# A fused layer on one core: the mixer's first projection moved ahead of its norm, with later residuals and wider steps in fox

## The chip, the cores and the metric

The kernel runs on one core of one Trainium2 chip. The metric is the device time of one execution in microseconds; lower is better. The engines are called as in the profile: PE (TensorE), DVE (VectorE), ACT (ScalarE), POOL (GpSimd), and SP (SyncE), whose queue issues the DMAs.

## The reference, cut to what matters

One decoder layer over 256 tokens with 2048 features, in float32. A conditioning vector c gives nine rows of 2048 (shift, scale and gate of each of three parts).

```
mod = silu(c) @ ada_w + ada_b                  # sh1 sc1 gt1 sh2 sc2 gt2 sh3 sc3 gt3
ada_in(x, g, shift, scale) = rmsnorm(x, g) * (1 + scale) + shift
x = x + 0.5 * gt1 * swiglu(ada_in(x, g0, sh1, sc1), w_gate0, w_up0, w_down0)    # d_ff 5632
x = x + gt2 * mixer(ada_in(x, g1, sh2, sc2))
x = x + 0.5 * gt3 * swiglu(ada_in(x, g2, sh3, sc3), w_gate1, w_up1, w_down1)
out = rmsnorm(x, final_norm)

mixer(h): one input projection gives, for heads of 128,
  8 heads of forgetting attention ("fox"): softmax(q k / sqrt(128) + cum_i - cum_j, causal) v,
      cum = cumsum(log_sigmoid(f + bias)); then rmsnorm
  8 heads of a gated delta rule ("gdn"): conv of width 4 and silu on q, k, v; q and k of unit length;
      g = -exp(A_log) * softplus(a + dt_bias), beta = sigmoid(b), in chunks of 64, each with a
      triangular solve; then rmsnorm times silu(z)
  o = concat(fox, gdn) @ w_out
```

## The kernel before, in words

**Weights.** All weights are one stream of 5392 tiles of 128x128, read in the order of use as 674 blocks of eight (W.block, W.next). For each block SP issues one DMA of 512 KB (wraw, L121), ACT rounds it to the high half (whi, L123) and DVE makes the low half, raw minus high (wlo, L135). The pools hold four blocks each. A product of one tile with 256 tokens is three matmuls: high by high, high by low, low by high. The activations (hs) are kept in halves too, in features by tokens.

**Stages.** FFN1 is blocks 0 to 263, in two halves of its inner width; each half has a stage for gate and up and a stage for down. The second half's down stage (blocks 232 to 263) has 16 output tiles of 16 products, each into a PSUM tile pd. The function after(j) inside ffn adds such a tile to the residual stream x (residual, two DVE steps, L509 and L510, with the gate's column gh, L507) and, in the second half, adds its squares for the next norm (sumsq_add, ACT and POOL). It is called when LATER products of the next tile are issued. Then come the mixer (input projections, heads, W_out), FFN2 and the final norm.

**Conditioning.** Each of the 140 later conditioning columns costs one DMA of 1 MB (adat, L256) and one DVE reduction (L260). They are dealt out along the weight stream: the table RATE gives, from a block on, how many columns fall due per block.

**A norm.** norm_sums turns the squares into sums per token (matmuls nsum, L323), with a square root on ACT and a few small DVE steps. norm_row puts the inverse root on every partition (matmul nrow, L342). modulate_one makes one of the sixteen h tiles: x g (1 + scale) times the row on DVE (ht, L368), shift and high half on ACT, low half on DVE (L372 or L376). Before the mixer, modulate does the sums and the row and leaves the tiles to h_need, which makes them a few ahead of the projection that uses them. Ahead of FFN2 the class Early does it in another way: during W_out it writes y = x g (1 + scale) into hs, the first products run on y with two more columns that hold the shift's halves (products, 258 columns), the sums and the row are issued among them (step), and root and shift are applied to the result (scaled, L433, with shc, L432). The h tiles for the later products are then made behind (h_upto).

**The mixer's order.** project runs the sixteen products of each item. The first call holds four items, interleaved: the gate columns gt and the key heads 0 to 2 of gdn. gates copies its columns to yr, transposes them (pcol, L811), runs a chain of small DVE steps, cumulates over tokens (prow, L844, and pcum), and writes the rows to DRAM (rowd). They come back on all partitions: four heads at a time for decays (fetch_rows, x<-rowd, L894), or one (row_of, rw<-rowd, L870). decays subtracts the rows (Ln, L902) and takes eight exponentials (L905); keys takes a key head's length and its inner products (pk, pkk, L934 to L941), solve the triangular solves. These chains are Python generators: each yield says for how many microseconds of products the chain rests. After a product, tick credits 0.35 us to every running chain, and a chain is resumed when its rest is used up. So all engines' programs are fixed at build time. fox is such a chain too: mask and logits (fm, L1147; plog), transposes (ppt, L1167), the product with v (pfo), the norm, and a transpose back (pft, L1189). ORDER lists the projections after the first: key heads 3 to 7, then z, v and the heads.

Of the kernel before, what the change touches and what calls it, by code (L numbers as in the profile page):

```python
# [16 lines left out]
P = 128  # L17
# [16 lines left out]
RATE = ((0, 0.5), (24, 0.34), (56, 0.45), (68, 0.06), (112, 0.5), (168, 0.38), (264, 0.0), (284, 0.26), (404, 0.0), (424, 0.125))  # L34
# [7 lines left out]
LATER = 8  # L42
# [107 lines left out]
def layer_kernel(ctx: ExitStack, tc: tile.TileContext, xrow, c, adaw, cols, cst, w, out, order, dbg=None):  # L150
# [204 lines left out]
    plain = hsf[:, : KD * HS].rearrange("p (k i) -> p k i", k=KD)[:, :, : 2 * T].rearrange("p k (q t) -> p k q t", q=2)  # L355

# [7 lines left out]
    def modulate_one(j, g1, sh, r, weave=True):  # L364

        t = pt("ht")
        hl, hh, tt = (run(j, LO), run(j, HI), turns(t)) if weave else (plain[:, j, LO], plain[:, j, HI], t)
# [17 lines left out]
    def modulate(which, m_sh, m_sc):  # L385
        ada_need(max(m_sh, m_sc), KD - 1)
        g1 = gains(which, m_sc, 0, KD)
        r = norm_row(norm_sums())
        hq["next"], hq["one"] = 0, lambda j: modulate_one(
            j, g1[:, j : j + 1], mod[:, m_sh * KD + j : m_sh * KD + j + 1], r, False)  # L390

    class Early:
# [3 lines left out]
        def __init__(self, which, m_sh, m_sc):  # L396
            self.which, self.m_sh, self.m_sc, self.row, self.rstd = which, m_sh, m_sc, None, None

        def y(self, j):
# [8 lines left out]
            A.activation(run(j, HI), turns(x[:, j]), AF.Copy, scale=g)  # L408
            V.scalar_tensor_tensor(run(j, LO), turns(x[:, j]), g, run(j, HI).bitcast(F32), ALU.mult, ALU.subtract)  # L409

        def step(self, k):
# [3 lines left out]
            if k == 4:  # L415
                self.row = norm_row(self.rstd, A.copy)
                g1 = gains(self.which, self.m_sc, 0, KD)
                hq["next"], hq["one"] = 0, lambda j: modulate_one(
                    j, g1[:, j : j + 1], mod[:, self.m_sh * KD + j : self.m_sh * KD + j + 1], self.row)
# [8 lines left out]
        def scaled(self, dst, ps):  # L428
# [4 lines left out]
            V.tensor_tensor(dst, ps[:, :T], self.row, ALU.mult)  # L433
# [181 lines left out]
    def ffn(which, m_gt, early=None):  # L615
        fs = list(range(NF))
        with tc.tile_pool(name=f"hid{which}", bufs=PARTS[which][1] + HIDX) as hp, \
                tc.tile_pool(name=f"more{which}", bufs=1) as more:
            W.more = more if MORE else None
            for half in range(2):  # L620
# [7 lines left out]
                def after(j):  # L628
                    residual(pds.pop(j), j, m_gt, True)
                    if half == 1:  # L630
                        sumsq_add(j)
                        if which == 1:
# [9 lines left out]
                for j in range(KD):  # L642
                    ps = psb("pd")
                    for q, hd in enumerate(hids):
                        if j and q == LATER:
# [77 lines left out]
    norm2 = Early(2, 6, 7)  # L723
# [5 lines left out]
    def mixer():  # L729
        modulate(1, 3, 4)  # L730
# [29 lines left out]
        def project(items):  # L760
# [3 lines left out]
            for i, k in todo:  # L764
                m, n = items[i]
                h_need(k)
                wh, wl = W.next(m, k, n)
                hh, hl = woven(plain[:, k, HI]), woven(plain[:, k, LO])
# [3 lines left out]
                tick(TILE_US)  # L772
            return [p_[:, :T] for p_ in pp]
# [671 lines left out]
```

## Time and profile before

| | |
|---|---|
| time, median of 3 runs | 1943.49 us (1943.44 to 1944.72) |
| the profiled execution's own time | 1943.79 us |
| its span in the trace | 1941.9 us |
| PE, DVE, ACT, POOL busy | 1903.0, 1554.0, 1041.2, 56.8 us |
| mean granted clock of PE | 0.992 |
| last pd matmul of FFN1 starts at | 741.19 us |

A line of the profile's timeline reads: start, duration, engine, line of the kernel, operation, output<-inputs, sizes, count, and in brackets how long the engine was idle before and which instruction ended that idle time. A line of a group reads: busy time, mean ns of one | idle time before them and what ended most of it. A line of the windows reads: from:to, length, then busy time and count of PE, weight loads, DVE, ACT and POOL, then the granted clock, the share of the DMA engines' time, and GB/s. A line of the waits reads: engine, what waited, what it waited for: total us, times, the longest.

### The profile page before, as it was taken

The numbers are of one execution on the slowest core, as the hardware profiler recorded it, in microseconds if no ns is written. First come the engines' busy times: TensorE is split into PE (matmuls) and PEld (weight loads), VectorE is DVE, ScalarE is ACT, GpSimd is POOL, SyncE is SP. The second block draws the span as 40 slices with busy tenths as digits, with TensorE's granted clock in tenths as the row PEclk, the third lists the DMA queues.
The fourth block names the chain that finished last, engine by engine and source line by source line (L and its number), as shares of the span: only waits on it lengthen the run. The fifth ranks groups of instructions, "written<-read, shape, count | busy, mean of one in ns | idle before, by whom it ended". The sixth has DMA issues, their size and how long they took to land. (4 is left out here: it accounts for less than half of the span.)

```text
span 1941.9 us, 33701 instructions
## 1 busy us (share of the span) xinstructions
PE 1903.0 (98%) x13087; PEld 1777.2 (92%) x13087; DVE 1554.0 (80%) x2415; ACT 1041.2 (54%) x1647; POOL 56.8 (3%) x55
## 2 busy tenths in 40 slices
PE   8999999999999999999999999999999999999998
PEld 6999999998999988889989998999999999999997
DVE  6999978989989997779987989976777665666654
ACT  6544555433455446858657655665554445555553
POOL 0000000000000030000000001100000000000011
PEclk8999999999999999999999999999999999999999
DMA  9989867999999975586667568667767665565663
GB/s 371 359 308 358 305 224 258 400 369 376 356 358 339 361 302 212 212 314 220 214 242 257 201 218 303 208 258 252 245 253 257 244 225 200 201 200 202 202 200 120
DMA packets 129490, 519.58 MB, mean 268 GB/s; under 512 B 18217, under 2 KB 21545, under 8 KB 111153
## 3 DMA queue, kind: packets, MB, share of 16 engines
q1 hardware_dynamic: 129330, 517.42, 72.9%
q8 instruction: 103, 1.69, 0.3%
q14 instruction: 57, 0.47, 0.1%
HBM read 512.89 MB, written 4.47 MB: 266 GB/s over the span
## 5 line engine op out<-in xcount | busy, mean ns | idle before, releaser
L135 DVE TENSOR_TENSOR wlo<-wraw,whi 128x1024 fp32r<-128x1024 f32 x674 | 822.3, 1226 | 268.3 <-ACT whi L123 267.3
L123 ACT CAST whi<-wraw 128x1024 fp32r<-128x1024 f32 x674 | 700.6, 1047 | 515.1 <-PE pd L485 166.5
L485 PE MATMUL pd<-hid,whi 128*128 128x512 f32 x1408 | 461.8, 382 | 0.0
L486 PE MATMUL pd<-hid,wlo 128*128 128x256 f32 x1408 | 384.6, 273 | 2.6 <-DVE wlo L135 2.6
L260 DVE CUSTOM_DVE_ANT_0 adat<-adat,cs,colt 128x2048 f32<-128x2048 f32 x140 | 329.2, 2351 | 6.5 <-DMA adat<-in_ada_dram 6.5
L481 PE MATMUL pg<-hs,whi 128*128 128x512 f32 x912 | 302.2, 382 | 0.5 <-DVE shc L432 0.5
L481 PE MATMUL pu<-hs,whi 128*128 128x512 f32 x912 | 302.2, 382 | 0.0
L485 PEld LDWEIGHTS pd<-hid,whi 128*128 128x128 f32 x1408 | 266.0, 189 | 36.9
L486 PEld LDWEIGHTS pd<-hid,wlo 128*128 128x128 f32 x1408 | 270.3, 192 | 5.4 <-DVE wlo L135 5.3
L567 PE MATMUL pgu<-hs,whi 128*128 128x256 f32 x896 | 245.8, 277 | 5.9 <-ACT hs L371 5.9
L482 PE MATMUL pu<-hs,wlo 128*128 128x256 f32 x912 | 249.2, 273 | 0.0
L482 PE MATMUL pg<-hs,wlo 128*128 128x256 f32 x912 | 248.9, 273 | 0.0
L569 PE MATMUL pgu<-hs,wlo 128*128 128x256 f32 x896 | 245.1, 278 | 2.4 <-DVE wlo L135 2.4
L568 PE MATMUL pgu<-hs,whi 128*128 128x256 f32 x896 | 246.5, 277 | 0.0
L481 PEld LDWEIGHTS pg<-hs,whi 128*128 128x128 f32 x912 | 172.4, 189 | 24.8 <-ACT shc L431 0.7
L481 PEld LDWEIGHTS pu<-hs,whi 128*128 128x128 f32 x912 | 172.4, 189 | 23.6
L769 PE MATMUL pp<-hs,whi 128*128 128x256 f32 x656 | 188.9, 289 | 1.6 <-ACT hs L375 1.6
L770 PE MATMUL pp<-hs,whi 128*128 128x256 f32 x656 | 182.9, 279 | 0.0
L771 PE MATMUL pp<-hs,wlo 128*128 128x256 f32 x656 | 182.7, 278 | 0.0
L567 PEld LDWEIGHTS pgu<-hs,whi 128*128 128x128 f32 x896 | 172.9, 194 | 6.7 <-ACT hs L371 6.3
L482 PEld LDWEIGHTS pu<-hs,wlo 128*128 128x128 f32 x912 | 175.0, 192 | 1.0 <-DVE wlo L135 0.9
L482 PEld LDWEIGHTS pg<-hs,wlo 128*128 128x128 f32 x912 | 175.1, 192 | 0.4
(337 smaller groups left out, 2593.8 us busy)
## 6 DMA issues: line engine op xcount, KB each, us to landing
wraw<-in_w_dram SPq DMA_DIRECT2D x674, 512.0 KB, 4.4
adat<-in_ada_dram SPq DMA_DIRECT2D x140, 1024.0 KB, 7.2
xr<-in_xr_dram SPq DMA_DIRECT2D x4, 512.0 KB, 5.3
adaf<-in_ada_dram SPq DMA_DIRECT2D x4, 512.0 KB, 8.5
adaf<-in_ada_dram SPq DMA_DIRECT2D x2, 1024.0 KB, 12.3
xd<-x SPq DMA_DIRECT2D x4, 512.0 KB, 7.0
rw<-rowd SPq DMA_DIRECT2D x16, 128.0 KB, 4.3
x<-xd SPq DMA_DIRECT2D x4, 512.0 KB, 5.8
```

Of the source, the lines that this page charges most:

```text
L123: self.cast = self.nc.scalar.copy(self.h, r).ins
L135: lo_ = nc.vector.tensor_tensor(self.l, r, self.h.bitcast(F32), ALU.subtract)
L260: V.tensor_tensor_reduce(t, t, cs, 1.0, L("adab", q, 1), ALU.mult, ALU.add, mod[:, q : q + 1])
L481: PE.matmul(ps, wt[0], both, start=(k == 0), stop=False)
L482: PE.matmul(ps[:, T:], wt[1], part(k, HI), start=False, stop=(k == KD - 1))
L485: PE.matmul(ps, wt[0], act.rearrange("p q (a b) -> p q b a", a=2), start=first, stop=False)
L486: PE.matmul(ps[:, :T], wt[1], woven(act[:, 0]), start=False, stop=last)
L567: PE.matmul(o, wh, part(k, HI), start=first and s == 0, stop=False, skip_group_check=skip)
L568: PE.matmul(o, wh, part(k, LO), start=False, stop=False, skip_group_check=skip)
L569: PE.matmul(o, wl, part(k, HI), start=False, stop=last, skip_group_check=skip)
L769: PE.matmul(pp[i][:, :T], wh, hh, start=(k == 0), stop=False)
L770: PE.matmul(pp[i][:, :T], wh, hl, start=False, stop=False)
```

## The change

- The class Early takes a view of the token order (runs or turns) and is used for the mixer's norm too, as norm1. FFN1's last down stage calls norm1.y(j) in after(j). The first call of project runs on y with 258 columns, the sums stand at its third k step and the row at its fifth. The gate columns and the three key heads of that call are scaled by the row and shifted after it (in gates and conv_silu). modulate and the layout "plain" of hs are gone, and later projections read hs through part.
- RATE: 0.42 instead of 0.38 columns per block from block 168 on, 0.24 from 232, none from 264, 0.29 from 288 (before: 0.26 from 284).
- LATER is a pair. In ffn the residual comes after product min(18, tile length - 2) of the next tile, so after 14 in FFN1's second half and 18 elsewhere; in W_out it stays 8.
- The last rest of decays is 3 instead of 1; the rests in fox are 1.5, 4.5, 1.5 and 6.5 instead of 1, 3, 1 and 5.

```diff
-RATE = ((0, 0.5), (24, 0.34), (56, 0.45), (68, 0.06), (112, 0.5), (168, 0.38), (264, 0.0), (284, 0.26), (404, 0.0), (424, 0.125))
+RATE = ((0, 0.5), (24, 0.34), (56, 0.45), (68, 0.06), (112, 0.5), (168, 0.42), (232, 0.24), (264, 0.0), (288, 0.29), (404, 0.0), (424, 0.125))
...
-LATER = 8
+LATER = (18, 8)
...
-    plain = hsf[:, : KD * HS].rearrange("p (k i) -> p k i", k=KD)[:, :, : 2 * T].rearrange("p k (q t) -> p k q t", q=2)
...
-    def modulate_one(j, g1, sh, r, weave=True):
+    def modulate_one(j, g1, sh, r, view=turns):
 
         t = pt("ht")
-        hl, hh, tt = (run(j, LO), run(j, HI), turns(t)) if weave else (plain[:, j, LO], plain[:, j, HI], t)
+        hl, hh, tt = run(j, LO), run(j, HI), view(t)
...
-    def modulate(which, m_sh, m_sc):
-        ada_need(max(m_sh, m_sc), KD - 1)
-        g1 = gains(which, m_sc, 0, KD)
-        r = norm_row(norm_sums())
-        hq["next"], hq["one"] = 0, lambda j: modulate_one(
-            j, g1[:, j : j + 1], mod[:, m_sh * KD + j : m_sh * KD + j + 1], r, False)
...
-        def __init__(self, which, m_sh, m_sc):
+        def __init__(self, which, m_sh, m_sc, view):
             self.which, self.m_sh, self.m_sc, self.row, self.rstd = which, m_sh, m_sc, None, None
+            self.view = view
...
-            A.activation(run(j, HI), turns(x[:, j]), AF.Copy, scale=g)
-            V.scalar_tensor_tensor(run(j, LO), turns(x[:, j]), g, run(j, HI).bitcast(F32), ALU.mult, ALU.subtract)
+            A.activation(run(j, HI), self.view(x[:, j]), AF.Copy, scale=g)
+            V.scalar_tensor_tensor(run(j, LO), self.view(x[:, j]), g, run(j, HI).bitcast(F32), ALU.mult, ALU.subtract)
...
                 hq["next"], hq["one"] = 0, lambda j: modulate_one(
-                    j, g1[:, j : j + 1], mod[:, self.m_sh * KD + j : self.m_sh * KD + j + 1], self.row)
+                    j, g1[:, j : j + 1], mod[:, self.m_sh * KD + j : self.m_sh * KD + j + 1], self.row, self.view)
...
-            V.tensor_tensor(dst, ps[:, :T], self.row, ALU.mult)
+            if self.view is turns:
+                V.tensor_tensor(dst, ps[:, :T], self.row, ALU.mult)
+            else:
+                V.tensor_tensor(runs(dst), turns(ps[:, :T]), runs(self.row), ALU.mult)
             return s[:, 1:]
...
                     residual(pds.pop(j), j, m_gt, True)
                     if half == 1:
                         sumsq_add(j)
-                        if which == 1:
+                        if which == 0:
+                            norm1.y(j)
+                        else:
...
-                        if j and q == LATER:
+                        if j and q == min(LATER[0], len(part) - 2):
                             after(j - 1)
...
-    norm2 = Early(2, 6, 7)
+    norm1, norm2 = Early(1, 3, 4, runs), Early(2, 6, 7, turns)
...
-        modulate(1, 3, 4)
...
-        def project(items):
+        def project(items, early=None):
 
             pp = [psn(i, "pp") for i in range(len(items))]
             todo = [(i, k) for k in range(KD) for i in range(len(items))]
             for i, k in todo:
                 m, n = items[i]
+                if early is not None:
+                    if i == 0:
+                        early.step(k)
+                    early.products(pp[i], W.next(m, k, n), k)
+                    continue
                 h_need(k)
                 wh, wl = W.next(m, k, n)
-                hh, hl = woven(plain[:, k, HI]), woven(plain[:, k, LO])
+                hh, hl = part(k, HI), part(k, LO)
                 PE.matmul(pp[i][:, :T], wh, hh, start=(k == 0), stop=False)
                 PE.matmul(pp[i][:, :T], wh, hl, start=False, stop=False)
                 PE.matmul(pp[i][:, :T], wl, hh, start=False, stop=(k == KD - 1))
                 tick(TILE_US)
+            if early is not None:
+                h_upto(KD)
+                return pp
...
-                    hh, hl = (plain[:, k, q, t * P : (t + 1) * P] for q in (HI, LO))
+                    hh, hl = (hs[:, k, q, t, :P] for q in (HI, LO))
...
         def gates(ps):
 
             yr = x[:, 8]
-            A.copy(runs(yr[R]), turns(ps[R]))
+            d = pt("ey")
+            s = norm1.scaled(d, ps)
+            A.activation(yr[R], d[R], AF.Identity, bias=s[R])
...
             for h in range(4 * half, 4 * half + 4):
                 for t in range(2):
                     A.activation(Ln[:, h, t], Ln[:, h, t], AF.Exp, bias=colS[:, t, 1, h : h + 1])
-            yield 1.0
+            yield 3.0
...
-        def conv_silu(ps, n, dst):
+        def conv_silu(ps, n, dst, early=None):
             cp, cv = pt("cp"), pt("cv")
             tap = lambda s: L("conv", 4 * n + s, 1)
-            A.copy(runs(cp), turns(ps))
+            if early is None:
+                A.copy(runs(cp), turns(ps))
+            else:
+                s = early.scaled(cp, ps)
+                A.activation(cp, cp, AF.Identity, bias=s)
             A.activation(cv, cp, AF.Copy, scale=tap(3))
-            for s in range(1, 4):
-                V.scalar_tensor_tensor(cv[:, s:], cp[:, : T - s], tap(3 - s), cv[:, s:], ALU.mult, ALU.add)
+            for d in range(1, 4):
+                V.scalar_tensor_tensor(cv[:, d:], cp[:, : T - d], tap(3 - d), cv[:, d:], ALU.mult, ALU.add)
             A.activation(dst, cv, AF.Silu)
...
             V.tensor_tensor(fm, fm, C("foxm"), ALU.add)
-            yield 1.0
+            yield 1.5
...
-            yield 3.0
+            yield 4.5
             ppt = psf("ppt")
...
-            yield 1.0
+            yield 1.5
             po = psf("pfo")
...
-            yield 5.0
+            yield 6.5
...
-        def have_keys(h, ps):
+        def have_keys(h, ps, early=None):
             kk[h] = otile("kk")
-            conv_silu(ps, NH + h, kk[h].bitcast(F32)[:, 0])
+            conv_silu(ps, NH + h, kk[h].bitcast(F32)[:, 0], early)
...
-        first = project([("gt", 0)] + [("qkv", NH + h) for h in range(3)])
+        first = project([("gt", 0)] + [("qkv", NH + h) for h in range(3)], norm1)
         start("k", -1, gates(first[0]))
         for h in range(3):
-            have_keys(h, first[1 + h])
+            have_keys(h, first[1 + h], norm1)
...
-                if owed and i == LATER:
+                if owed and i == LATER[1]:
                     owed.pop(0)()
```

PE at the start of the mixer. pd is the last down tile of FFN1, nsum and nrow are the norm's sums and row, pp the accumulators of the first projection. Before:

```order
L485 MATMUL pd<-hid,whi 128x512
L486 MATMUL pd<-hid,wlo 128x256
L323 MATMUL nsum<-colt,sqacc 128x2 x2
L323 MATMUL nsum<-colt,sq 128x2 x2
L342 MATMUL nrow<-colt,rb 128x128 x2
L769 MATMUL pp<-hs,whi 128x256 x4
L770 MATMUL pp<-hs,whi 128x256
L771 MATMUL pp<-hs,wlo 128x256
```

After, from the last pd to the first products, and then the place of the sums:

```order
L480 MATMUL pd<-hid,whi 128x512
L481 MATMUL pd<-hid,wlo 128x256
L416 MATMUL pp<-hs,whi 128x258
L417 MATMUL pp<-hs,whi 128x256
L418 MATMUL pp<-hs,wlo 128x258
L416 MATMUL pp<-hs,whi 128x258
```

```order
L416 MATMUL pp<-hs,whi 128x258
L417 MATMUL pp<-hs,whi 128x256
L418 MATMUL pp<-hs,wlo 128x258
L323 MATMUL nsum<-colt,sqacc 128x2 x2
L323 MATMUL nsum<-colt,sq 128x2 x2
L416 MATMUL pp<-hs,whi 128x258
L417 MATMUL pp<-hs,whi 128x256
```

The sums moved from directly behind the last down product to behind eight products of the first projection; the row's matmul stands nine products further on, behind row L418 there.

ACT around the first exponentials of decays (Ln), where pk is a key head's accumulator, read by L940 and L941 (L950 and L951 afterwards), fm fox's mask from the row rw, and kk<-cv a head's silu. Before:

```order
L940 ACTIVATE j_8994,ssk<-pk 128x128
L940 ACTIVATE j_8996,ssk<-pk 128x128
L941 COPY kk<-pk 128x256
L1047 ACTIVATE kbd<-kk,colS 128x128
L123 CAST whi<-wraw 128x1024
L1147 ACTIVATE fm<-rw,colS 128x128
L905 ACT_TABLE_LOAD
L905 ACTIVATE Ln<-Ln,colS 128x128 x8
L922 ACT_TABLE_LOAD
L922 ACTIVATE kk<-cv 128x256
L940 ACTIVATE j_9047,ssk<-pk 128x128
```

After:

```order
L950 ACTIVATE j_9159,ssk<-pk 128x128
L950 ACTIVATE j_9161,ssk<-pk 128x128
L951 COPY kk<-pk 128x256
L1157 ACTIVATE fm<-rw,colS 128x128
L1157 ACTIVATE fm<-rw,colS 128x256
L123 CAST whi<-wraw 128x1024
L911 ACT_TABLE_LOAD
L911 ACTIVATE Ln<-Ln,colS 128x128 x8
L932 ACT_TABLE_LOAD
L932 ACTIVATE kk<-cv 128x256
L950 ACTIVATE j_9206,ssk<-pk 128x128
```

The reading of the second key head's pk stood behind the exponentials (the last row before) and stands ahead of them now; the mask's second piece and one more cast have come in between, ahead of the exponentials.

SP's queue, where rowd is the DRAM copy of the rows, xd the copy of x, and wraw a weight block. Before:

```order
L751 DMA xd<-x 128x1024 x3
L121 DMA wraw<-in_w_dram 128x1024 x5
L751 DMA xd<-x 128x1024
L121 DMA wraw<-in_w_dram 128x1024 x15
L856 DMA rowd<-x 8x512
L121 DMA wraw<-in_w_dram 128x1024 x2
L894 DMA x<-rowd 128x4x256
L870 DMA rw<-rowd 128x256 x2
```

After:

```order
L747 DMA xd<-x 128x1024 x3
L121 DMA wraw<-in_w_dram 128x1024 x7
L747 DMA xd<-x 128x1024
L121 DMA wraw<-in_w_dram 128x1024 x15
L862 DMA rowd<-x 8x512
L121 DMA wraw<-in_w_dram 128x1024 x2
L900 DMA x<-rowd 128x4x256
L876 DMA rw<-rowd 128x256 x2
```

The write of the rows and the reads behind it stand two weight blocks later: seven instead of five blocks lie between the two issues of xd, and 15 between the second and the rows in both.

## The prediction

> **What bounds the kernel now.** I read the head of the page, then what TensorE (PE) waited for, then the timeline at its largest waits.
>
> ```profile
> span 1941.9 us, 33701 instructions
> PE 1903.0 (98%) x13087; PEld 1777.2 (92%) x13087; DVE 1554.0 (80%) x2415; ACT 1041.2 (54%) x1647; POOL 56.8 (3%) x55
> ...
> engine line waited for: us in total, times, longest us
> ...
> PE pkk L937 <- ACT kk L941: 2.7, 1, 2.7
> PE pd L486 <- DVE wlo L135: 2.6, 9, 0.6
> ...
> PE ppt L1167 <- ACT x L1162: 1.3, 2, 1.1
> ```
>
> PE is busy for 98% of the span, and no product is taken away. So the change can only win back waits of PE and stretches at a lowered clock. The largest group stands where the mixer begins:
>
> ```profile
> 741.30 0.51 PE L323 MATMUL nsum<-colt,sqacc 128*128 128x2 f32 x4
> 743.07 0.61 PE L323 MATMUL nsum<-colt,sq 128*128 128x2 f32 x4 [1.26 <-ACT sq L309]
> 745.20 0.71 PE L342 MATMUL nrow<-colt,rb 128*128 128x128 f32 x4 [1.53 <-DVE rb L341]
> 747.46 0.80 PE L769 MATMUL pp<-hs,whi 128*128 128x256 f32 x2 [1.55 <-ACT hs L375]
> ...
> 746.76:753.59 6.83, 6.13 (x28) 6.13 (x29) 6.24 (x15) 3.81 (x8) 0.42 (x2) 0.50 0.22 77
> 753.59:788.40 34.81, 34.81 (x312) 34.65 (x310) 28.72 (x66) 29.71 (x52) 0.00 (x0) 1.00 0.49 173
> 807.60:815.03 7.43, 4.70 (x17) 3.77 (x17) 4.52 (x13) 7.41 (x20) 0.00 (x0) 0.77 0.23 76
> 682.00:738.00 56.00, 55.06 (x333) 49.88 (x332) 52.11 (x67) 25.50 (x34) 14.95 (x11) 1.00 0.83 317
> ```
>
> The first four lines are PE's chain for the norm: sums, row, first product, each waiting for the one before. The last four are windows: length, busy time of PE, weight loads, DVE, ACT and POOL, then the granted clock. After the waits the clock is 0.50 for 6.83 us; around the wait at pkk it is 0.77 over 7.43 us, which is 1.7 us lost (0.23 x 7.43). The second line gives the pace: 312 matmuls in 34.81 us, so 0.112 us each and 0.336 us for a product of three.
>
> **A, the norm leaves the path.** The waits removed are 1.26 + 1.53 + 1.55 = 4.34 us; the window at half clock did in 6.83 us what 3.41 us would do. Together 7.75 us. Products now run over y = x g (1 + scale), and the sums and the row stand among them. The row's matmul still needs DVE's root, for which I count 0.35 us of wait (0 to 1.5, what it waits today).
>
> **B, the gates come later.** Today ACT copies the gate columns as soon as the first projection ends. After the change they are scaled by the row, so they need the row and whatever DVE has ahead of them. DVE still makes the sixteen h tiles for the later projections, at these prices:
>
> ```profile
> L135 DVE TENSOR_TENSOR wlo<-wraw,whi 128x1024 fp32r<-128x1024 f32 x7 | 8.5, 1220 | 0.0
> L368 DVE SCALAR_TENSOR_TENSOR ht<-x,g,nrow 128x256 f32<-128x256 f32 x16 | 7.1, 478 | 0.0
> L376 DVE SCALAR_TENSOR_TENSOR hs<-ht,mod,hs 128x256 fp32r<-128x256 f32 x8 | 3.9, 481 | 0.0
> L372 DVE TENSOR_TENSOR hs<-ht,hs 128x256 fp32r<-128x256 f32 x8 | 3.4, 424 | 2.5 <-ACT hs L371 2.5
> ...
> L433 DVE TENSOR_TENSOR tg<-pg,nrow 128x256 f32<-128x256 f32 x3 | 1.3, 418 | 0.0
> ...
> L921 DVE SCALAR_TENSOR_TENSOR cv<-cp,colt,cv 128x255 f32<-128x255 f32 (+2 forms) x14 | 6.2, 473 | 0.0
> ...
> 775.02 0.30 PE L811 MATMUL pcol<-colt,x 24*128 24x24 f32 x2
> ...
> 788.51 0.39 PE L844 MATMUL prow<-cstt,x 128*8 128x128 f32 x2
> ```
>
> I count from t = 0 at 741.30. The row is ready at about 8. In DVE's order 32 steps for h (14.4 us by these busy times), seven low halves (8.5), four scalings (1.7) and seven convolution steps (3.1) stand ahead of the end of the gates' scaling: 27.7 us. Neighbouring instructions overlap in these rows (16 of 478 ns make 7.1 us, not 7.6), and two or so of the low halves fall before the row, so I take 25: the scaled gates at 33, ACT's shift on them at 34. PE reaches pcol, now 24 products behind the first projection, at 31.8: a wait of 2.3 us. Two more DVE chains (gates interleaved with convolutions) then end at 49.4, where PE would come to prow at 47.6: 1.8 us. The new waits make 0.35 + 2.3 + 1.8 = 4.45, so A and B give 7.75 - 4.45 = **-3.3 us**. The ends: no new wait but the row's, -7.4; DVE's full 27.7 and another half-clock window behind the wait at pcol (1.7), -0.3 or, with as much again at prow, +1.5.
>
> A cross-check: prow stands at t = 47.2 today; afterwards at 49.4, but 16 products (5.4 us) further on in PE's program. That is 3.2 us won.
>
> **C, the first keys.** The wait of 2.73 us at pkk has its cause on ACT:
>
> ```profile
> 803.72 0.40 ACT L1147 ACTIVATE fm<-rw,colS 128x128 f32<-128x128 f32 x1 [2.30 <-DMA rw<-rowd]
> 804.13 1.28 ACT L905 ACT_TABLE_LOAD   x1
> 805.43 2.45 ACT L905 ACTIVATE Ln<-Ln,colS 128x128 f32<-128x128 f32 x8
> 807.88 1.28 ACT L922 ACT_TABLE_LOAD   x1
> ...
> 810.00 0.37 ACT L941 COPY kk<-pk 128x256 f32<-128x256 f32 x1
> ...
> 810.42 0.71 PE L937 MATMUL pkk<-kk 128*128 128x128 f32 x4 [2.73 <-ACT kk L941]
> ```
>
> The rows arrive 15.2 us after prow (803.72 against 788.51). Then a forget-mask step, a table load, eight exponentials and another load keep ACT from reading the second key head's pk, and pkk of the third head waits until that reading is done. Afterwards the second pk is read ahead of all this, so its wait goes. The same chain now delays the reading of the third pk, for which the fourth pkk, 18 products later than today's, waits in turn. The chain begins at 49.4 + 14.6 = 64 (the writing and reading of the rows moved with prow past two weight blocks on SP's queue; I take 0.6 off since part of the 15.2 is waiting in that queue), and grows from 6.7 us (803.72 to 810.42) by a second mask piece (0.5) and a cast (1.05) to 8.25. It ends at 72.2. PE is there at 66.4 (807.69, where today's wait begins) - 3.3 + 6.0 (18 products) = 69.1. The wait would be 3.1 instead of 2.73, with the same loss of clock: **+0.4 us**. Ends: -4.4 (2.73 and 1.7 both gone) and +4.8 (3.1 us more of wait, and half of one more window of 3.41 us). The Trainium skill, in TensorE: Matmul & The Clock Gate (the section Why this matters for your kernels), warns of gaps in PE's work above about 3 us, since an idle window puts the clock back to half. Here the half clock followed a gap of 2.73 us already, so the measurement decides; by the rule, a wait that stays below the 3 us would cost no clock, and the sum would be 1.7 us lower.
>
> The Trainium skill, in ScalarE: Activation LUTs (What ACT_TABLE_LOAD costs), puts a switch of tables at about 1.28 us and another 1.38 us of drain. The rows show 1.28 with the next ACTIVATE 0.02 us behind it, at 805.43, so I count no drain; by the page's figure the two switches would add 2.8 us to this wait if only the new place of the chain paid them.
>
> **D, fox.** The wider steps put the transposes (ppt) five products later behind their logits. PE's 1.3 us of waiting at ppt (quoted above) came from the second half's decays:
>
> ```profile
> 866.73 1.23 DVE L902 TENSOR_TENSOR Ln<-cstt,x 128x1024 f32<-128x1024 f32 x1 [2.36 <-DMA x<-rowd]
> ```
>
> DVE stood 2.36 us for the rows. Their fetch is issued three blocks earlier now, and the five products add 1.7 us of cover. Both hide it: **-1.3 us** (-2.9 with the 1.4 us at pft, +1.5 if the mask rows come late instead).
>
> **E, residuals at product 14 or 18 of the next tile.** Today, at product 8, DVE waits at them in its order:
>
> ```profile
> 457.94 0.48 DVE L509 SCALAR_TENSOR_TENSOR x<-pd,gh,x 128x256 f32<-128x256 f32 x1 [1.32 <-PE pd L486]
> ...
> 460.51 1.05 ACT L123 CAST whi<-wraw 128x1024 fp32r<-128x1024 f32 x1 [2.88 <-DMA wraw<-in_w_dram]
> ```
>
> Low halves queue behind that, and PE's nine waits for them in pd cost 2.6 us. Later residuals wait less, but ACT's 2.88 us for a weight block shows that part is the transfer's. I take **-1.0 us** (-2.6 to +1.0).
>
> **F, FFN1's last down stage carries y.** These are its groups on DVE in 54 us (ten tiles), and the price of y in the stage of W_out, which makes it already:
>
> ```profile
> L135 DVE TENSOR_TENSOR wlo<-wraw,whi 128x1024 fp32r<-128x1024 f32 x22 | 29.0, 1329 | 1.1 <-ACT whi L123 1.1
> L260 DVE CUSTOM_DVE_ANT_0 adat<-adat,cs,colt 128x2048 f32<-128x2048 f32 x6 | 14.9, 2479 | 0.0
> ...
> L409 DVE SCALAR_TENSOR_TENSOR hs<-x,g,hs 128x256 fp32r<-128x256 f32 x16 | 13.9, 874 | 0.3 <-ACT hs L408 0.3
> ...
> L382 DVE SCALAR_TENSOR_TENSOR g<-mod,colt 128x1 f32<-128x1 f32 (+1 forms) x15 | 2.7, 185 | 0.2
> ```
>
> A tile of 16 products takes 5.38 us, of which DVE is busy 93% (52.11 of 56.00, quoted above): 0.37 us free. y and its gain add 0.87 + 0.19. The lower rate takes four of eleven conditioning steps out of the stage, 4 x 2.48 / 16 = 0.62 a tile. Net 0.44, or 0.07 more than is free; over 15 tiles 1.0, of which the buffers made ahead hide some: **+0.6 us** (0 to +9.8). The three steps that the higher rate adds ahead of it spread 7.4 us of DVE over 64 blocks of 2.69 us, 4%, within the 7% free: nothing.
>
> **Sum.** -3.3 + 0.4 - 1.3 - 1.0 + 0.6 = -4.6. The profiled execution took 1943.79 us (span 1941.9), 0.3 above the median 1943.49; from the median that is 1938.9.
>
> **Rivals.** *The gates never make PE wait.* If DVE does the h steps in its gaps and rows come earlier, B costs only the row's 0.35, and the chain of C ends before PE comes: -7.4 - 4.4 - 1.3 - 0.4 = -13.5, 1930.0. For it: DVE waits 2.5 us for ACT among the h steps today, so it has slack; against it: 27.7 us of queued DVE work. *The gain comes back at the keys.* The rows come no earlier while PE does, so the fourth pkk waits some 5.8 us and a second window runs at half clock: C is +4.8, and -3.3 + 4.8 - 1.3 - 0.4 leaves -0.2, 1943.3. For it: the chain on ACT grows by 1.55 us. *Slower: DVE starves PE while it makes y.* Each y waits on DVE for ACT's high half, which can stand behind a 1.05 us cast, and low halves queue behind it. An excess of 0.75 us a tile over 13 tiles (the first three use what is made ahead) is 9.8 instead of 0.6: +4.6, 1948.1. It decides from about 0.7 us a tile; W_out's stage waited just 0.3 us in all for that half, but has more free DVE time.
>
> **How the numbers follow.** Differences within 0.2% (3.9 us) can't be told from none here. My forecast gets 0.42, with its own range 1934 to 1944: 0.27 faster, 0.15 same. The first rival gets 0.27 (faster), the second 0.14 (same), the third 0.17 (slower). The range 1929.0 to 1946.5 leaves out most of the slower case and a little below the first rival.
>
> **What would show it.** In the profile after: no wait at the mixer's first product, and a clock of 1.00 there (A); waits of PE at pcol and prow of 2.3 and 1.8 us (B), near zero for the first rival; the largest wait still at a pkk, the fourth head's, of about 3 us (C), over 5 for the second rival; none at the first ppt (D); PE's waits for wlo in the down stages below 2 us together (E), and DVE near 100% in the last 80 us before the mixer with under 1 us of waiting there (F), some 10 us for the third rival. I am wrong if PE waits anywhere in the first projection, or if pcol alone takes more than 5 us.

## The result: no difference, and where the gain went

The changed kernel takes 1943.78 us (median of 12 runs, 1941.27 to 1947.06), the kernel before 1943.22 (12 runs, 1939.76 to 1944.72). The ratio is 1.0007, 95% interval 0.9998 to 1.0016: the same within the 0.2% named above, and 4.9 us above the forecast. The profiled execution took 1943.93 us.

The head of the page after:

```profile
span 1942.1 us, 33819 instructions
PE 1903.3 (98%) x13087; PEld 1775.5 (91%) x13087; DVE 1565.9 (81%) x2456; ACT 1047.4 (54%) x1668; POOL 53.1 (3%) x55
```

PE's waits after (what waited, for what, total us, times, longest us):

```profile
PE pp L770 <- DVE shc L424: 2.7, 1, 2.7
...
PE po L480 <- ACT whi L123: 2.1, 2, 1.2
PE pd L481 <- DVE wlo L135: 1.7, 6, 0.6
PE po L481 <- DVE wlo L135: 1.7, 2, 1.4
```

The three waits at the norm and the 2.7 us at pkk are gone from the list. In their place stand one wait at pp, the first product of the fourth key head, and four in W_out (po). The timeline of PE at the start of the mixer:

```profile
741.35 0.27 PE L481 MATMUL pd<-hid,wlo 128*128 128x256 f32 x1
741.45 0.28 PE L416 MATMUL pp<-hs,whi 128*128 128x258 f32 x1
...
767.28 0.48 PE L770 MATMUL pp<-hs,whi 128*128 128x256 f32 x1 [2.69 <-DVE shc L424]
...
777.23 0.30 PE L817 MATMUL pcol<-colt,x 24*128 24x24 f32 x2
...
790.83 0.39 PE L850 MATMUL prow<-cstt,x 128*8 128x128 f32 x2
```

Windows of the same kernel (length; busy PE, weight loads, DVE, ACT, POOL; then the clock):

```profile
741.45:767.36 25.91, 23.22 (x207) 22.94 (x206) 23.16 (x52) 19.46 (x40) 1.74 (x7) 1.00 0.50 164
767.36:770.77 3.41, 3.41 (x17) 3.41 (x18) 3.41 (x9) 2.15 (x7) 0.00 (x0) 0.50 0.93 234
1160.00:1180.00 20.00, 16.52 (x88) 14.06 (x87) 16.91 (x31) 9.42 (x16) 3.29 (x3) 0.91 0.56 202
```

The first projection follows FFN1's last product at once and runs at full clock. The 2.69 us at its end bring one window at half clock (1.7 us lost). In W_out, 3.5 us of a 20 us window are idle and the clock is 0.91.

Where the time went is best read from the start times of the same operations in both timelines. The fourth column is what the line adds to the difference of after minus before (negative is a gain); at prow and at the fourth head's pkk it also takes into account the products that now stand ahead of them (15.7 and 6 more, at 0.336 us). Each trace is one execution. Three kernels whose programs are the same between the fourth pkk and W_out (the changed one and two of those below) took 327.1, 326.9 and 326.2 us there, so a step of less than 1 us is not clear of this spread.

| operation on PE | before, us | after, us | step, us |
|---|---|---|---|
| last product of FFN1 | 741.19 | 741.35 | +0.2 |
| prow | 788.51 | 790.83 | -3.1 |
| fourth head's pkk | 816.76 | 811.87 | -4.0 |
| first product of W_out | 1143.67 | 1138.99 | +2.2 |
| first product of FFN2 | 1234.67 | 1234.88 | +4.9 |
| end of the span | 1941.9 | 1942.1 | 0.0 |

So 7.1 us are won by the fourth key head. 2.2 of them are lost among the heads and 4.9 in W_out. DVE's timeline in W_out, after:

```profile
1165.84 2.35 DVE L260 CUSTOM_DVE_ANT_0 adat<-adat,cs,colt 128x2048 f32<-128x2048 f32 x1 [2.45 <-DMA adat<-in_ada_dram]
1168.12 0.09 DVE L260 DVE_READ_ACCUMULATOR2_ANT mod<- 128x1 f32 x1
1168.12 0.87 DVE L504 SCALAR_TENSOR_TENSOR x<-po,mod,x 128x256 f32<-128x256 f32 x2
...
1172.66 1.21 DVE L135 TENSOR_TENSOR wlo<-wraw,whi 128x1024 fp32r<-128x1024 f32 x1
1173.80 1.82 DVE L401 SCALAR_TENSOR_TENSOR hs<-x,g,hs 128x256 fp32r<-128x256 f32 x2
1175.54 2.34 DVE L260 CUSTOM_DVE_ANT_0 adat<-adat,cs,colt 128x2048 f32<-128x2048 f32 x1
...
1178.27 1.21 DVE L135 TENSOR_TENSOR wlo<-wraw,whi 128x1024 fp32r<-128x1024 f32 x1
```

A conditioning step that waits 2.45 us for its transfer, the residuals of the first four tiles, their y, and a second conditioning step stand close together. The low half before these rows starts at 1161.16; between it and 1178.27 there is one other. PE uses up a block in 2.69 us (eight products), so four blocks made ahead don't last. The same place before:

```profile
1168.75 2.35 DVE L260 CUSTOM_DVE_ANT_0 adat<-adat,cs,colt 128x2048 f32<-128x2048 f32 x1 [0.79 <-DMA adat<-in_ada_dram]
...
1171.02 1.22 DVE L135 TENSOR_TENSOR wlo<-wraw,whi 128x1024 fp32r<-128x1024 f32 x1
1172.16 0.87 DVE L509 SCALAR_TENSOR_TENSOR x<-po,mod,x 128x256 f32<-128x256 f32 x2
...
1187.87 2.32 DVE L260 CUSTOM_DVE_ANT_0 adat<-adat,cs,colt 128x2048 f32<-128x2048 f32 x1
```

There the step waits 0.79 us, a low half stands between it and the residuals, and the next step comes 19 us later instead of 9.7.

### The profile page after: what moved, and what is told of

The parts are those of the page before. It is cut to its first block, busy times and chain, and to the rows that moved or that the text cites. A ratio compares the mean times of both kernels' runs of the same rounds, so it can differ in the third digit from the quotient of the medians.

```text
span 1942.1 us, 33819 instructions
## 1 busy us (share of the span) xinstructions
PE 1903.3 (98%) x13087; PEld 1775.5 (91%) x13087; DVE 1565.9 (81%) x2456; ACT 1047.4 (54%) x1668; POOL 53.1 (3%) x55
## 4 chain that ended last, share of the span: by engine, by line
PE 44%; DVE 5%; issue 2%; ACT 1%; DMA 0%; DVEq 0%; SPq 0%; ACTq 0%
PE pd L480 8%; PE pg L476 7%; PE pu L476 7%; PE pd L481 4%; PE pu L477 4%; PE pg L477 4%; DVE wlo L135 1%; DVE adat L260 1%; PE po L480 1%; PE pp L770 1%; PE pp L772 1%; PE pp L771 1%; PE pv L786 1%; PE pv L788 1%; PE pv L787 1%
## 5 line engine op out<-in xcount | busy, mean ns | idle before, releaser
L562 PEld LDWEIGHTS pgu<-hs,whi 128*128 128x128 f32 x896 | 172.8, 194 | 6.7 <-ACT hs L369 6.3
L564 PEld LDWEIGHTS pgu<-hs,wlo 128*128 128x128 f32 x896 | 172.0, 194 | 3.3 <-DVE wlo L135 3.3
L770 PE MATMUL pp<-hs,whi 128*128 128x256 f32 x592 | 171.6, 290 | 2.7 <-DVE shc L424 2.7
L563 PEld LDWEIGHTS pgu<-hs,whi 128*128 128x128 f32 x896 | 173.3, 194 | 0.2 <-DVE hs L370 0.2
```

Of the source, the lines that this page charges most:

```text
L562: PE.matmul(o, wh, part(k, HI), start=first and s == 0, stop=False, skip_group_check=skip)
L563: PE.matmul(o, wh, part(k, LO), start=False, stop=False, skip_group_check=skip)
L564: PE.matmul(o, wl, part(k, HI), start=False, stop=last, skip_group_check=skip)
L770: PE.matmul(pp[i][:, :T], wh, hh, start=(k == 0), stop=False)
```

## Experiments

Each is an edit of the changed kernel unless it says otherwise. Ratios are against the kernel before, with 95% intervals.

**No conditioning in W_out.** Is the loss there the work on DVE, or do the transfers (x comes back, beside the weights) give the time?

```diff
-(264, 0.0), (288, 0.29), (404, 0.0), (424, 0.125))
+(264, 0.0), (288, 0.37), (380, 0.0), (424, 0.125))
```

> The changed kernel with one edit in RATE: 0.37 columns per block from 288 and none from 380 (W_out begins near 378) until 424. Theory P: the 4.7 us that are won by the start of W_out are lost there because on DVE a conditioning step, waiting for its DMA, and the residuals of the first four tiles stand between two low halves. Without conditioning there W_out loses under 1 us in waits instead of 3.5 and no clock, and the time is 1938 to 1940. Theory T: W_out's start is bound by its transfers (x comes back, 2 MB, beside the weights), so what is won earlier is waited for there: waits of 3 us or more remain, and the time is 1942.5 to 1944. Against both: seven columns made earlier may cost waits among the heads, up to 2 us.

1940.89 us, ratio 0.9996 (0.9987 to 1.0005). From its first product to FFN2's, W_out takes 88.6 us, against 91.0 before and 95.9 after. But W_out starts at 1143.73, no earlier than before: the columns made earlier cost the heads 5.1 us (from the fourth pkk to W_out 332.2 us instead of 327.1), well over the 2 us allowed for. So the total, between the two expected ranges, doesn't settle it. The stage speaks for the conditioning columns as the cause; their transfers went together with their work on DVE, so it doesn't tell these two apart.

**The norm's change alone**: RATE, LATER and the rests of decays and fox as before.

> The changed kernel with RATE, LATER (8 and 8) and the rests of decays and fox as before, so only the norm's change is left. If the norm's change alone carries the gain of 4 to 7 us by the fourth key head and the other numbers cost the 2.6 us among the fox heads and the 4.9 us of W_out: 1937 to 1940. If W_out takes back whatever comes earlier (theory T), or the order there is the norm's own doing (on DVE the conditioning step stands directly ahead of the four residuals in this kernel too, where one low half lay between before): 1942 to 1944, with waits of 3 us or more in W_out's first tiles.

1946.12 us, ratio 1.0026 (1.0016 to 1.0036): slower by 0.26%, which neither expectation had. The loss is in a stage that they left out. Its windows on the last down stage of FFN1, and those of the kernel before and after:

```profile
688.00:738.00 50.00, 46.51 (x278) 41.55 (x277) 49.86 (x76) 25.77 (x39) 14.15 (x9) 1.00 0.81 297
```

```profile
688.00:738.00 50.00, 49.37 (x300) 44.90 (x299) 46.11 (x61) 23.20 (x31) 13.88 (x10) 1.00 0.84 321
```

```profile
688.00:738.00 50.00, 50.00 (x307) 45.97 (x306) 49.65 (x78) 27.91 (x41) 10.20 (x9) 1.00 0.83 288
```

With y and the old rate DVE is busy for 49.86 of 50 us and PE for 46.51: the stage takes 90.6 us instead of 85.5. PE waits there for gains and low halves, as these rows of its timeline show:

```profile
726.13 0.38 PE L481 MATMUL pd<-hid,wlo 128*128 128x256 f32 x1 [0.81 <-DVE gh L502]
...
732.58 0.38 PE L481 MATMUL pd<-hid,wlo 128*128 128x256 f32 x1 [0.94 <-DVE wlo L135]
```

This is the third rival's mechanism, held off in the changed kernel by the lower rate. From FFN1's end to W_out this kernel takes 397.9 us, as after (397.6; before 402.5), and its W_out 91.2. So the norm's change by itself wins about all that is won between FFN1 and W_out, and W_out's loss isn't its doing.

**All but the norm's change**: the kernel before with the new RATE, LATER and rests.

> The kernel before with the changed kernel's RATE, LATER and rests, without the norm's change. Theory P: W_out has the changed kernel's order of transfers, so it loses about 5 us there, and the fox heads lose 2.6: 1946 to 1951. Theory T: PE comes to W_out no earlier than before, so nothing is waited for there; only the fox heads' part remains: 1943 to 1946. The wait at the fourth key head's pkk (2.73) shows whether the rest of 3 after decays removes it without the norm's change: gone if the rest does it, 2 to 3 us if not.

1944.28 us, ratio 1.0012 (1.0003 to 1.0022): in theory T's range, but not by T's path, which had PE come to W_out no earlier and lose nothing there. W_out takes 95.2 us. PE comes there 2.9 us earlier than before and loses 4.2, so more than is won earlier: W_out doesn't just wait for the same moment. The wait at pkk is 0.8 us instead of 2.73, without the norm's change; the loss among the heads is 0.2 us, not the 2.6 expected. From FFN1's end to W_out this kernel takes 398.8 us: each half of the change wins some 4 us there by itself (402.5 before), and both together (397.6) hardly more. Set beside the norm's change alone, whose W_out takes 91.2 us, DVE's conditioning steps there show what differs. First the norm's change alone, then this kernel:

```profile
1170.86 2.35 DVE L260 CUSTOM_DVE_ANT_0 adat<-adat,cs,colt 128x2048 f32<-128x2048 f32 x1 [0.97 <-DMA adat<-in_ada_dram]
...
1189.98 2.32 DVE L260 CUSTOM_DVE_ANT_0 adat<-adat,cs,colt 128x2048 f32<-128x2048 f32 x1
```

```profile
1166.03 2.35 DVE L260 CUSTOM_DVE_ANT_0 adat<-adat,cs,colt 128x2048 f32<-128x2048 f32 x1 [1.37 <-DMA adat<-in_ada_dram]
...
1175.82 2.34 DVE L260 CUSTOM_DVE_ANT_0 adat<-adat,cs,colt 128x2048 f32<-128x2048 f32 x1
```

In both the first step stands directly ahead of the four residuals, with waits of 0.97 and 1.37 us. The second comes 19.1 us later in the one and 9.8 in the other. That points to the second step, close behind the first, as the larger part of the loss.

**Another PSUM bank for the fourth key head**, so that its first product doesn't wait for the scaling.

```diff
-        def project(items, early=None):
+        def project(items, early=None, bank=0):
-            pp = [psn(i, "pp") for i in range(len(items))]
+            pp = [psn(bank + i, "pp") for i in range(len(items))]
...
-                have_keys(h, project([("qkv", NH + h)])[0])
+                have_keys(h, project([("qkv", NH + h)], bank=N_BIG if h == 3 else 0)[0])
```

> The changed kernel with the fourth key head's projection in a PSUM bank of the other pool, so that it doesn't wait for the scaling of the first projection's banks. The wait of 2.69 us at its first product and the half clock behind it (1.7) go. If nothing stands behind it, prow comes 4.4 us earlier and the time is 1939 to 1940. If DVE's queue is the bound (gates scaled at 774.7 in the changed kernel), PE comes to pcol at 772.8 and waits there for about 3 us, and prow gains under 1.5 us: 1942.5 to 1944.

1947.30 us, ratio 1.0033 (1.0020 to 1.0046): slower, also outside both expectations. The median is of 5 runs, and the profiled execution is the longest of them (1951.41 us). The wait at pp is gone, and prow comes 5.0 us sooner after FFN1's end (44.45 us instead of 49.49). But in this kernel 9.7 products fewer stand ahead of prow, which is 3.2 us; so 1.8 us are won, near the second expectation (under 1.5). At the fourth pkk nothing is left of it: 70.43 us behind FFN1's end, 70.52 after. The waits move on. A row of PE's timeline, one of its waits, and the window behind that wait:

```profile
777.79 0.30 PE L817 MATMUL pcol<-colt,x 24*128 24x24 f32 x2 [1.66 <-ACT x L808]
```

```profile
PE ppt L1177 <- ACT x L1172: 3.8, 1, 3.8
```

```profile
869.00:875.83 6.83, 6.08 (x28) 5.41 (x27) 6.17 (x7) 6.08 (x18) 0.00 (x0) 0.50 0.65 209
```

PE waits 1.66 us at pcol (3 expected), 2.2 at pkk and 3.8 at the first ppt, with two windows at half clock behind it. The heads take 332.6 us. PE reaches W_out 2.0 us later than before, and W_out takes 96.7 us. That refutes theory T as the first expectation puts it: here nothing was won ahead of W_out, and it still loses 5.7.

**A pause around W_out's first residuals only.**

```diff
-(288, 0.29), (404, 0.0), (424, 0.125))
+(288, 0.29), (388, 0.0), (400, 0.3), (406, 0.0), (424, 0.15))
```

> The changed kernel with one edit in RATE: no columns fall due from block 388 to 400 (before that 0.29 as in the changed kernel, then 0.3 to block 406, 0.15 from 424). The earlier no-columns kernel showed W_out 7.3 us shorter than the changed kernel's, but its seven columns made earlier cost the heads what had been won there. Here no column is made earlier. Of the two conditioning steps that stand on DVE around the first four tiles' residuals one is left. If these two steps cost W_out its 4.9 us, the heads keep the changed kernel's lead (W_out starts near 1139.0), W_out takes 91 us or less, and the time is 1938 to 1940. If W_out can't run earlier because its transfers bound it, it takes 94 to 96 us and the time is 1942.5 to 1944.

1938.75 us, ratio 0.9984 (0.9975 to 0.9993): the fastest of all, ahead of both kernels. W_out starts at 1139.13 and takes 91.1 us; the span is 1937.5. DVE there:

```profile
1163.98 1.23 DVE L135 TENSOR_TENSOR wlo<-wraw,whi 128x1024 fp32r<-128x1024 f32 x1 [0.45 <-ACT whi L123]
1165.12 0.87 DVE L504 SCALAR_TENSOR_TENSOR x<-po,mod,x 128x256 f32<-128x256 f32 x2
...
1169.83 2.33 DVE L260 CUSTOM_DVE_ANT_0 adat<-adat,cs,colt 128x2048 f32<-128x2048 f32 x1
...
1174.29 1.21 DVE L135 TENSOR_TENSOR wlo<-wraw,whi 128x1024 fp32r<-128x1024 f32 x1
```

One conditioning step is left, without a wait, and a low half is made just ahead of the residuals. One wait of 1.81 us remains on PE, at full clock. This recovers 4.8 of the 4.9 us, as expected. Against the kernel before, the 0.16% lie within the 0.2% that the prediction counts as none, though the interval leaves out 1.

**x read back later**: is it the late transfer or the work?

```diff
-BACK = (4, 6, 9)
+BACK = (4, 7, 10)
```

> The changed kernel with BACK (4, 7, 10) for (4, 6, 9): the third and fourth piece of x are read back two blocks later in W_out, so that the transfer of the conditioning column beside them has less company. DVE's order around the first four tiles' residuals is unchanged, with both conditioning steps. If the late transfer (7.4 us for the column, a DVE wait of 2.45) is what costs W_out its 4.9 us, W_out takes 91 to 92.5 us and the time is near 1940. If it is the two steps' 4.7 us on DVE between the low halves, W_out still takes 94 to 96 us and the time is 1942.5 to 1944.

1943.67 us, ratio 1.0008 (0.9999 to 1.0017); W_out takes 96.6 us. DVE's order is the changed kernel's, and the column lands no sooner, as its timeline shows:

```profile
1165.70 2.35 DVE L260 CUSTOM_DVE_ANT_0 adat<-adat,cs,colt 128x2048 f32<-128x2048 f32 x1 [2.84 <-DMA adat<-in_ada_dram]
```

So the piece of x that was moved is not what delays the column. The time falls to the second expectation, the steps' work, and the stage just above its range. How the 4.9 us divide exactly between that wait and the two steps stays open, since no run removed the wait alone; the pair of kernels above, with 91.2 and 95.2 us, puts most of it on the second step.

**The pause with fox's old rests.**

> The kernel with the pause in W_out, and the rests of fox as before (1, 3, 1, 5); the rest of 3 after decays stays. If the wider rests save waits of PE in fox (1.3 us predicted), this kernel is 1 to 2 us slower than the one with the pause alone; if the 2.2 us that the changed kernel loses between the fourth head and W_out come from the wider rests, it is up to 2 us faster.

1943.88 us, ratio 1.0009 (1.0000 to 1.0018), 0.25% above the pause alone and more than either expectation had. Of the 3.7 us between the spans, 2.6 are in W_out (93.7 us), whose order moves with the rests, and 0.7 among the heads (327.6 against 326.9 us). There PE waits 2.7 us at the first plog, where it waits 1.1 with the wider rests. So the old rests don't make the heads any faster, and the wider ones don't cause the 2.2 us lost. That they are worth 0.7 us there is not shown: kernels with the same program in that stretch differ by 0.9.

**An even rate in FFN1's second half.**

```diff
-(168, 0.42), (232, 0.24), (264, 0.0)
+(168, 0.36), (264, 0.0)
```

> The changed kernel with 0.36 columns per block from 168 to 264 in place of 0.42 and then 0.24: as many columns in all, but some four more in FFN1's last down stage. Only the end of FFN1 is read here (741.35 in the changed kernel). If the lower rate is what keeps DVE from starving PE there, FFN1 ends 5 to 9 us later, with waits of PE at residual gains and low halves in that stage. If the later residuals do it, it ends under 1.5 us later.

A single run, 1946.06 us; only its stages are read. The down stage takes 87.5 us (83.8 after), and the first projection then waits for the last tile's y:

```profile
745.89 0.35 PE L416 MATMUL pp<-hs,whi 128*128 128x258 f32 x1 [1.96 <-DVE x L505]
```

That is 3.6 + 2.0 = 5.6 us, in the range. But the stage for gate and up ahead of it is shorter by 2.6 us (167.7 against 170.3), so FFN1's end moved by 1.1 us only. Read at that end, as the expectation has it, the result falls to the other side (under 1.5 us); that place was badly chosen, since the stages ahead of it change too.

**Residuals after 8 products**, with the changed kernel's other numbers and then with the pause as well.

> The changed kernel with the residuals after 8 products in FFN1 and FFN2 as before. Read at the end of FFN1 (741.35) and of FFN2 (the last products start at 1929.5, 694.7 us after W_out's last). If the later residuals are worth the 1 us that was predicted, FFN1 ends 0.5 to 1.5 us later; if DVE's load alone decides, under 0.3.

> The kernel with the pause in W_out, and the residuals after 8 products as before. The look at 8 products alone showed FFN1's down stage at 83.84 us, as with 14, and the heads 2 us shorter than in the changed kernel. If the later residuals are worth nothing, this kernel has no conditioning step around the first residuals (the low halves stand closer there), W_out takes 90 to 91.5 us and the time is 1935.5 to 1938. If they are worth what was predicted (1 us), it is at 1939 or above, by waits in the down stages.

A single run took 1940.63 us; with the pause it is 1939.60 us, ratio 0.9990 (0.9981 to 0.9999), not to be told from the pause with late residuals. By its total the second falls to the side on which the later residuals are worth 1 us (1939 or above); FFN1's stages say otherwise. The down stage takes 83.84 us in both, as with 14 products. FFN1's end at 742.49 isn't 1.1 us of stage time: its down stage starts at 658.65, 1.1 us later, from the stages ahead. So the later residuals are worth nothing in FFN1. In FFN2 the kernel without the pause loses nothing either (from its first product to the end 707.2 us, 707.3 after), while the kernel with the pause takes 708.9 there, with one wait of 1.39 us for DVE at the first down stage; whether the 8 products alone cause that is open. The heads take 325.4 and 325.3 us, some 1.7 less than after, and W_out takes 93.8 us without the pause, 2.1 less than after; neither was taken apart.

## Why the prediction was right or wrong

The time lies in the range and at "same", which had 0.29. The likeliest case did not happen, and the second rival's total (1943.3) came out with another mechanism. That is luck. Up to W_out the gain was 4.7 us, where the forecast had 4.6, but its terms were off in both directions; and W_out, which had no term, then took it back.

**A was right**: products start 0.1 us behind FFN1, at clock 1.00. **B was right in its sum, wrong in its place.** prow came at t = 49.4 as worked out, and the step is -3.1 us for -3.3. But there is no wait at pcol or prow. The step that failed is "The new waits make 0.35 + 2.3 + 1.8": I asked when the gates are ready, and not who takes the banks of the first projection next. The fourth key head does, and DVE's scaling of a bank stands behind h steps and two low halves; it waits 2.69 us and loses 1.7 to the clock, 4.4 in all for my 4.45. That the sizes agree is chance: 1.7 of it is clock, which my 4.45 does not hold. The bank's kernel bears out at pcol that the DVE work queued there is a limit: the gates' scaling starts 34.2 us behind FFN1's end there (33.4 after), and PE waits for it. Its waits at pkk and ppt stand behind the rows from DRAM instead (ACT's mask step waits 1.93 us for them).

**C was wrong**: -4.0 us for +0.4, close to what the first rival had for it (-4.4). Its ACT chain took what was worked out (8.0 us for 8.25), but began 12.4 us behind prow, and not 14.6:

```profile
803.19 0.80 ACT L1157 ACTIVATE fm<-rw,colS 128x128 f32<-128x128 f32 x2
...
804.95 1.28 ACT L911 ACT_TABLE_LOAD   x1
806.24 2.45 ACT L911 ACTIVATE Ln<-Ln,colS 128x128 f32<-128x128 f32 x8
808.70 1.28 ACT L932 ACT_TABLE_LOAD   x1
...
810.82 0.37 ACT L951 COPY kk<-pk 128x256 f32<-128x256 f32 x1
```

The third pk is read by 811.2, and PE comes to the fourth pkk at 811.87 without a wait.

Before, SP issued a conditioning column of 1 MB 0.05 us behind the reads of the rows, as its timeline shows:

```profile
794.97 0.98 SPq L870 DMA_DIRECT2D rw<-rowd  x2
796.00 0.52 SPq L256 DMA_DIRECT2D adat<-in_ada_dram  x1
```

After, RATE pauses until block 288, and the next column is issued two weight blocks behind them. I counted the move of this boundary from 284 to 288 as nothing; that it lets the rows land sooner fits these rows but was not tried by itself. It isn't needed for most of the gain: the kernel with the norm's change alone has the old boundary and the old rest, its mask step starts 13.3 us behind prow, and its wait at the third pkk is 0.92 us at full clock, so it wins 3.2 of the 4.0. The drain that the Trainium skill adds to a table load (ScalarE: Activation LUTs, What ACT_TABLE_LOAD costs) did not show: the exponentials started 0.01 us behind a load of 1.28 (804.95 to 806.24).

**D was wrong in sum**: +2.2 us among the heads for -1.3. The old waits at ppt are gone, but plog waits 1.1 us and low halves 1.5 more. Without the norm's change the same rests lose 0.2; with the norm's change and the old rests 1.8 are lost (0.7 of a product more stands ahead of the pkk there). So the loss goes with the norm's change and not with the rests. PE comes earlier there while the rows and columns do not; that this is why is argued from the waits, and the two kernels with residuals after 8 products, which lose only 0.5, leave the cause open.

**E was wrong**: nothing in FFN1, for -1.0 (and FFN2 takes 707.3 us before and after). **F was wrong in sign**: the down stage is 1.6 us shorter than before (83.8 for 85.5) instead of 0.6 longer, because four columns fewer outweigh y: with the new rate the stage takes 83.8 us without y too (in the kernel with all but the norm's change), and with y at the old rate 90.6. The stage ahead of it, where I counted the higher rate as nothing, is 1.6 longer (170.3 for 168.7 us). Windows inside it, before and after:

```profile
488.00:654.00 166.00, 166.00 (x1009) 151.75 (x1008) 151.29 (x176) 83.67 (x125) 0.00 (x0) 1.00 0.92 353
```

```profile
488.00:654.00 166.00, 165.72 (x1000) 150.36 (x999) 154.42 (x182) 82.11 (x124) 0.00 (x0) 1.00 0.96 363
```

DVE is busy 154.42 us instead of 151.29 and PE gets through 1000 matmuls instead of 1009, though it counts as busy throughout: it lags in waits too short for the list. At 0.36, 0.38 and 0.42 columns per block that stage takes 167.7, 168.7 and 170.3 us; the two kernels with half of the change each confirm it (168.7 at 0.38, 170.3 at 0.42). The 7% of free DVE time that I counted on had been measured in another stage.

**W_out was no term at all.** Its 4.9 us are what made a gain into no difference. The columns' place there was part of the change: with the old numbers W_out takes 91.0 and 91.2 us, with the new ones 95.2 to 96.7 in four kernels (93.8 with the even rate and with residuals after 8 products), and the pause takes it to 91.1 (93.7 with fox's old rests). Which step stands where thus depends on the rests too; RATE was not changed by itself. The forecast counted how many columns the new rates make, and did not follow where they fall.

## What to carry to other kernels

When a step is deferred to the end of an accumulation, ask who needs the accumulator's bank next, not only who needs the value. When a table of rates changes, follow each transfer and its compute step to the place where it now falls, to the end of the program; a step costs where it lands in an engine's order, far from the edit. A stage in which an engine is nearly full (here DVE, 99% in the down stage) can hold new work only if other work leaves it, and where that goes has its own price.

## What the runs showed of the hardware

The half clock follows some waits and not others of the same size. It came behind the wait at the fourth head's first product in the changed kernel (2.69 us) and in five of its variants (2.53 to 2.69), but not in the even rate's and the two with residuals after 8 products, whose wait there was 2.68 or 2.69 too. Nor did it come behind 2.71 at plog in the kernel with the pause and fox's old rests, or behind 2.91 at pft in the one without columns in W_out. Shorter waits differ in the same way: it came behind 1.88 us (at 861.24, without columns in W_out) and not behind 1.95 (at 1179.48, with the pause and the old rests). Each stretch at half clock behind a wait lasted 3.41 us, or twice that. The Trainium skill (TensorE: Matmul & The Clock Gate, What's actually happening) tells of a free-running window of about 3.4 us, and says of the speeding up that it depends on where in the window the first matmul lands. The lengths agree. That slowing down depends in the same way on where a wait falls is my inference; equal waits with different outcomes fit it. In a sum of terms, a wait near 2.7 us thus costs either itself or 1.7 us more, and the trace of before can't say which.
